# Modulation sums placed in layer 0, input sums with a margin, and silu as one ScalarE function

## The chip, the cores and the metric

The kernel runs on one core of one Trainium2 chip. A core has five engines that run side by side, each with its own queue of instructions in order: TensorE (PE, with its weight loads as PEld), VectorE (DVE), ScalarE (ACT), GpSimd (POOL) and SyncE (SP), which here issues the DMA transfers. The metric is the device time of one execution in microseconds (us); before the change it is 1677.81 us, the median of three runs.

## What is computed

Two layers of a transformer block act on two streams of 256 tokens, `x` and `ctx`. Each layer is a feed-forward, a mixing step (attention and pooling), and a second feed-forward; in the last layer `ctx` stops before the second half. Norms are scaled and shifted by modulation vectors, which come from a matrix of 1024 x 9216 in each layer.

```python
def rms_norm(x, g):
    xf = x.astype(jnp.float32)
    y = xf * lax.rsqrt(jnp.mean(xf * xf, axis=-1, keepdims=True) + RMS_EPS)
    return (y * g.astype(jnp.float32)).astype(x.dtype)

def modulate(h, shift, scale):
    return h * (1.0 + scale) + shift

def mod_vectors(cvec, w_mod, b_mod):
    m = jax.nn.silu(cvec) @ w_mod + b_mod
    return jnp.split(m, N_MOD, axis=-1)

def swiglu(h, w_gate_up, w_down):
    gate, up = jnp.split(h @ w_gate_up, 2, axis=-1)
    return (jax.nn.silu(gate) * up) @ w_down

def sandwich_ffn(x, w_gate_up, w_down, g_pre, g_post, shift, scale, gate):
    h = modulate(rms_norm(x, g_pre), shift, scale)
    return x + 0.5 * gate * rms_norm(swiglu(h, w_gate_up, w_down), g_post)
```

`D_MODEL` is 1024, `D_FF` 2816 (22 blocks of 128), `N_MOD` 9, `DEPTH` 2.

## The kernel before

**Numbers as pairs.** Each operand of a matmul is kept as a high and a low part; a product is three matmuls (`mm3`). To split a tile, ACT copies the high part and DVE subtracts it from the source to get the low part (`split`). Weights arrive by DMA in `raw` tiles of 1 MB and become two `w` tiles each (`Stream.prep`), so every weight costs one ACT and one DVE pass.

**Stages.** `ffn(0, 0)`, `token_mix(0)`, `ffn(0, 1)`, `ffn(1, 0)`, `token_mix(1)`, `ffn(1, 1)` run one behind the other. A feed-forward goes through its 22 blocks in groups (8, 8 and 6; in `ffn(1, 0)` 4, 4, 4, 4 and 6). Each group first makes the gate and up sums of its blocks (`pg`, `pu`) and their products (`product`, then `split` into `g`), and then multiplies `g` by the down weights into `pd`, which is added to `y`. Behind the last group, `close` does the norm of a token tile and prepares the next stage's input `h`; POOL takes the powers of the norms (`power`, `rs`).

**Seven products.** `ffn(1, 0)`, layer 1's first feed-forward, computes most blocks with seven quarter products in place of eight (`gate_up_seven`). It needs sums of weight quarters, which POOL makes from `raw` (`prep_seven`: `s12`, `s34`), and sums of input quarters, also on POOL (`Input.add_up`: from `yg` tiles, split into `ht`). Its first three blocks use the plain product, by halves of the tokens (`columns_half`). The quarter products land in banks `p1`, `p26`, `p57`, `p34` and are put together by DVE in `u` and `c`.

**Modulation.** The vectors of layer 0 for the first norm are made at the start by PE. All others are 16 jobs of nine steps (`mod_steps`): eight times a load of 0.5 MB (`wm`) and a multiply-add on DVE for each stream into `acc`, then `last`: DMAs that fold `acc` into `part`, three additions on POOL, a small matmul (`pm`) and, for gates, a transpose (`pr`). The last four jobs, of layer 1's second half, have one stream. `fill(rate)` behind each block of a feed-forward releases `rate` further steps; `debt` carries the fraction. There are 144 steps; 22 blocks at 2.6 release 57.

**What sets the order.** The whole program is first recorded and then ordered by a planner (`Recorder.order`): each engine's next instruction is the one that could start first by the planner's own prices, ties broken by the recorded order. `rec.margin` adds a time to the moment from which an instruction counts as ready. The order is fixed when the program is built; on the chip every engine takes its queue in that order and waits on semaphores. Places are limited: 16 large tiles (`w`, `g`, `h`), 2 `raw`, 10 working tiles (`wm`, `acc`, `part`, `tt`, `s12` among them), 8 PSUM banks.

All instructions of the recorded program carry one line number in the profile, L382 (`issue`), so groups are told apart by tile names.

Of the kernel before, what the change touches and what calls it, by code (L numbers as in the profile page):

```python
# [13 lines left out]
AF = mybir.ActivationFunctionType  # L14
ALU = mybir.AluOpType
# [10 lines left out]
EPS = 1e-6  # L26
# [9 lines left out]
LEAD = 3  # L36
# [1 line left out]
BLOCK = 4  # L38
PLACES = {"big": 16, "raw": 2, "wk": 10, "ps": 8, "st": 24}
LIMITS = {"ps": 1}  # L40
RATE = 2.6
BEHIND = 0
MARGIN = 6.0
HASTE = 0.5
# [4 lines left out]
XS, CS, ALL = slice(0, S), slice(S, N_TOK), slice(0, N_TOK)  # L49
# [350 lines left out]
def tile_dit_block(  # L400
# [36 lines left out]
    def wtile(shape, base="wk", dtype=F32):  # L437
        return rec.tile("wk", shape, dtype, base)
# [18 lines left out]
    class Stream:  # L457
        def __init__(self):
            self.plan = []
            self.ready = []  # L460
            self.raws = []
            self.taken = 0
            self.ahead = AHEAD

        def add(self, src, parts, seven=False):
            self.plan.append((src, parts, seven))
# [23 lines left out]
        def prep_seven(self, raw):  # L490

            (a11, a12), (a21, a22) = ((raw[:, i, 0:512], raw[:, i, 512:D]) for i in range(2))
            s12, s34 = wtile([P, 2, 512], "s12"), wtile([P, 2, 512], "s34")
            nc.gpsimd.tensor_add(s12[:, 0, :], a21, a22)
            nc.gpsimd.tensor_sub(s12[:, 1, :], s12[:, 0, :], a11)
            nc.gpsimd.tensor_sub(s34[:, 0, :], a11, a21)
            nc.gpsimd.tensor_sub(s34[:, 1, :], a12, s12[:, 1, :])
            wa = slot([P, 2, D], "w")
            split(wa[:, 0, :], wa[:, 1, :], raw[:, 0, :])
            w12 = slot([P, 2, D], "w")  # L500
            split(w12[:, 0, :], w12[:, 1, :], s12.rearrange("p a c -> p (a c)"))
            self.ready.append((wa, w12))
            w34 = slot([P, 2, D], "w")
            split(w34[:, 0, :], w34[:, 1, :], s34.rearrange("p a c -> p (a c)"))
            wb = wtile([P, 2, 512], "wb", F32R)
            split(wb[:, 0, :], wb[:, 1, :], a22)
            self.ready.append((w34, wb))
# [201 lines left out]
    def fill(n):  # L709

        debt[0] += n
        rec.delay = BEHIND
        while debt[0] >= 1 and todo:
            steps = todo[0][1]
            steps.pop(0)()
            debt[0] -= 1
            if not steps:
                todo.pop(0)
        rec.delay = 0
# [18 lines left out]
    def power(sq, eps):  # L738

        st = stat(2, "rs")  # L740
        nc.gpsimd.tensor_scalar(
            out=st[:, 0:1], in0=sq[:, 0:1], scalar1=sq[:, 1:2], scalar2=eps, op0=ALU.add, op1=ALU.add
        )
        nc.gpsimd.tensor_tensor(out=st[:, 1:2], in0=st[:, 0:1], in1=nhalf, op=ALU.pow)
        return st[:, 1:2]
# [4 lines left out]
    class Input:  # L750
# [21 lines left out]
        def add_up(self):  # L772

            self.sums = [slot([P, 2, 4, S], "ht") for _ in range(4)]
            lower, upper = slice(0, 4), slice(4, KD)
            for o in range(2):
                one, two = self.full[ORDER[o]], self.full[ORDER[2 + o]]
                a, b, c, d = one[:, lower, :], two[:, lower, :], two[:, upper, :], one[:, upper, :]
                nc.gpsimd.tensor_sub(a, b, a)
                nc.gpsimd.tensor_sub(b, c, b)  # L780
                nc.gpsimd.tensor_sub(c, c, a)
                nc.gpsimd.tensor_sub(d, d, c)
                for i, src in enumerate((a, c, b, d)):
                    dst = self.sums[i][:, :, :, o * P : (o + 1) * P]
                    split(dst[:, 0], dst[:, 1], src)
            self.full = {}
# [65 lines left out]
    def close(t, pd, y, half, nxt, Hn):  # L852

        n = wtile([P, D], "n")
        yg = wtile([P, D], "yg")
        sq, sx = stat(2, "sq"), stat(2, "sx")
        rec.haste = HASTE
        for h, hc in enumerate(HALVES):
            src = pd[h]
            if y is not None:  # L860
                src = y[:, hc]
                nc.vector.tensor_add(src, src, pd[h])
            square(n[:, hc], src, sq[:, h : h + 1], 1.0 / 16.0 if half else 1.0 / 32.0)
            nc.vector.tensor_mul(yg[:, hc], src, gbc[t // 2][:, hc])
        r = power(sq, 16.0 * EPS if half else EPS)
        for h, hc in enumerate(HALVES):
            nc.vector.scalar_tensor_tensor(
                out=X[t][:, hc], in0=yg[:, hc], scalar=r, in1=X[t][:, hc], op0=ALU.mult, op1=ALU.add
            )
            if nxt is None:  # L870
                nc.sync.dma_start(out=out[0, t * P : (t + 1) * P, hc], in_=X[t][:, hc])
            else:
                square(n[:, hc], X[t][:, hc], sx[:, h : h + 1])
        if nxt is not None:
            normed(t, nxt[0], nxt[1], n, yg.rearrange("p (k c) -> p k c", k=KD), Hn, sx)
        rec.haste = 0.0
# [45 lines left out]
    def ffn(l, ff, both, nxt, rate, lead, parts):  # L922
# [12 lines left out]

        def product(tt, pg, pu):

            nc.scalar.activation(tt[:, 0, :], pg, AF.Tanh, scale=0.5)
            nc.vector.scalar_tensor_tensor(out=tt[:, 1, :], in0=tt[:, 0, :], scalar=1.0, in1=pg, op0=ALU.add, op1=ALU.mult)
            nc.vector.tensor_mul(tt[:, 0, :], tt[:, 1, :], pu)  # L940

        def gate_up_evac(f, pg, pu):
# [7 lines left out]
        def gate_up(fs, parts):  # L950
            held = []
            for f in fs:
                held.append((f, ws.get(), ws.get(), bank("pg"), bank("pu")))
            for part in parts:
                for f, wg, wup, pg, pu in held:
                    if seven:
                        columns_half(pg, wg, part)
                        columns_half(pu, wup, part)
                    else:
                        columns(pg, wg, part)  # L960
                        columns(pu, wup, part)
                    if part is parts[-1]:
                        gate_up_evac(f, pg, pu)
                if seven and part is parts[0]:
                    H["now"].add_up()

        def gate_up_seven(f):

# [43 lines left out]
        for gi, (f0, f1) in enumerate(groups):  # L1012
            f = f0
            if gi == 0 and parts is None:
                by_token()
                f = BLOCK
            elif gi == 0:
                gate_up(tuple(range(lead)), parts)
                f = lead
                fill(lead * rate)  # L1020
            while f < f1:
                if seven:
                    gate_up_seven(f)
                else:
                    gate_up((f,), (cs,))
                f += 1
                fill(rate)
            if gi + 1 < len(groups):
                for h in range(2):
                    hc = slice(h * 512, (h + 1) * 512)  # L1030
# [342 lines left out]

    ffn(0, 0, True, (0, 3), RATE, START, (CS, XS))
    token_mix(0, (0, 6))
    ffn(0, 1, True, (1, 0), RATE, LEAD, (CS, XS))
    ffn(1, 0, True, (1, 3), RATE, LEAD, (0, 1))
    token_mix(1, (1, 6))
    ffn(1, 1, False, None, 0.0, 0, None)

    with tc.manual_schedule():
        rec.issue(tc.nc, rec.order(), {tag: psum if tag == "ps" else pool for tag in PLACES})
# [103 lines left out]
```

## Time and profile before

| | us |
|---|---|
| median of 3 runs | 1677.81 (1677.76 to 1678.05) |
| the profiled execution's own time | 1681.01 |
| its span, first to last instruction | 1679.1 |

The stages in the profiled execution, as the first matmuls of each in PE's timeline show them:

| stage | begins about, us |
|---|---|
| `ffn(0, 0)` | 38 |
| `token_mix(0)` | 401 |
| `ffn(0, 1)` | 606 |
| its second and third group | 743 and 876 |
| `ffn(1, 0)` | 982 (its first seven-product block 1021) |
| `token_mix(1)` | 1347 |
| `ffn(1, 1)` | 1483 |

A row of a group or a timeline names the engine, the operation, and `out<-in` by tiles with buffer numbers left out; `[4.76 <-ACT g_big L382]` means that the engine stood idle for 4.76 us before it and that ACT's writing of `g` ended the wait. Matmuls are pipelined and their ends are modelled, so time lost on PE is better read from the distance between starts than from its busy share.

### The profile page before, as it was taken

Reading aid. Unit: us, or ns where it says so; the run is one execution under the profiler, and the core shown is the slowest. Engines: PE = TensorE matmul, PEld = TensorE weight load, DVE = VectorE, ACT = ScalarE, POOL = GpSimd, SP = SyncE. Lnnn points to the kernel's source line nnn. Section 1 sums busy time; section 2 is a strip of 40 time slices with the busy share of each in tenths; the row PEclk is TensorE's granted clock in tenths of the full one; section 3 lists DMA queues with packets and bytes.
Section 4 is the critical chain, followed back from the end, with each engine's and each line's share of the span. In section 5 each row is a group of like instructions: output and inputs, shape, how many; then the busy total and the mean of one; then the engine's idle time right before and its main releaser. Section 6 shows DMA issues by size and latency. Waiting matters only on the chain.

```text
span 1679.1 us, 23648 instructions
## 1 busy us (share of the span) xinstructions
PE 1624.4 (97%) x9074; PEld 1396.6 (83%) x9074; DVE 1276.3 (76%) x1748; ACT 729.0 (43%) x1287; POOL 363.7 (22%) x348
## 2 busy tenths in 40 slices
PE   6999999999999999999999988999999999899998
PEld 4988888888877798888888888979889888779997
DVE  7987876556789689967745499899989788975664
ACT  7422322225566562232222273433434567664442
POOL 1011111102133211120110064362754022210000
PEclk9999999999999999999999999999999999999999
DMA  9467656631222425765554216354323412355551
GB/s 377 165 233 245 226 176 217 200 104 66 89 73 86 158 101 206 249 212 202 197 187 164 100 42 230 132 187 168 121 101 105 163 57 100 123 199 191 201 197 57
DMA packets 98960, 269.11 MB, mean 160 GB/s; under 512 B 9424, under 2 KB 39328, under 8 KB 87072
## 3 DMA queue, kind: packets, MB, share of 16 engines
q1 hardware_dynamic: 98848, 267.60, 45.7%
q8 instruction: 72, 1.18, 0.3%
q14 instruction: 40, 0.33, 0.1%
HBM read 251.80 MB, written 1.09 MB: 151 GB/s over the span
## 4 chain that ended last, share of the span: by engine, by line
PE 74%; DVE 12%; ACT 5%; issue 3%; DMA 2%; POOL 2%; SPq 1%; POOLq 0%; DVEq 0%; ACTq 0%
PE pd_ps L382 22%; PE pg_ps L382 19%; PE pu_ps L382 19%; PE p_ps L382 6%; DVE w_big L382 3%; PE pk_ps L382 2%; PE pv_ps L382 2%; ACT n_wk L382 2%; POOL rs_st L382 2%; PE pq_ps L382 1%; DVE acc_wk L382 1%; DMA w_big<-in_wmod_dram 1%; ACT sx_wk L382 1%; DVE tt_wk L382 1%; PE pt_ps L382 1%
## 5 line engine op out<-in xcount | busy, mean ns | idle before, releaser
L382 DVE TENSOR_TENSOR w_big<-raw_raw,w_big 128x1024 fp32r<-128x1024 f32 x293 | 374.5, 1291 | 103.2 <-ACT w_big L382 102.5
L382 PE MATMUL pd_ps<-w_big,g_big 128*128 128x512 f32 x1848 | 437.6, 397 | 9.9 <-ACT g_big L382 7.0
L382 PEld LDWEIGHTS pd_ps<-w_big,g_big 128*128 128x128 f32 x1848 | 347.9, 189 | 91.5 <-ACT g_big L382 7.9
L382 ACT ACTIVATE w_big<-raw_raw 128x1024 fp32r<-128x1024 f32 x293 | 302.6, 1053 | 230.9 <-DMA raw_raw<-in_wgu_dram 92.2
L382 PE MATMUL pu_ps<-h_big,w_big 128*128 128x512 f32 (+1 forms) x1944 | 367.8, 342 | 0.0
L382 PEld LDWEIGHTS pu_ps<-h_big,w_big 128*128 128x128 f32 x1944 | 305.6, 189 | 42.6
L382 PE MATMUL pg_ps<-h_big,w_big 128*128 128x512 f32 (+1 forms) x1752 | 331.0, 343 | 2.6 <-ACT h_big L382 1.7
L382 PEld LDWEIGHTS pg_ps<-h_big,w_big 128*128 128x128 f32 x1752 | 276.0, 189 | 43.6 <-ACT h_big L382 2.6
L382 DVE SCALAR_TENSOR_TENSOR acc_wk<-wm_wk,csil,acc_wk 128x1024 f32<-128x1024 f32 x196 | 249.5, 1307 | 41.4 <-DMA wm_wk<-in_wmod_dram 41.3
L382 POOL TENSOR_TENSOR part_wk<-part_wk 128x512 f32<-128x512 f32 (+2 forms) x84 | 89.5, 1066 | 474.6 <-DMA part_wk<-acc_wk 380.8
L382 ACT ACTIVATE g_big<-tt_wk 128x512 fp32r<-128x512 f32 (+1 forms) x84 | 49.2, 585 | 285.5 <-DVE tt_wk L382 283.5
L382 POOL TENSOR_SCALAR rs_st<-sq_st 128x1 f32<-128x1 f32 x24 | 8.3, 346 | 521.0 <-ACT n_wk L382 520.9
L382 POOL TENSOR_TENSOR s_wk<-raw_raw 128x512 f32<-128x512 f32 x38 | 67.4, 1784 | 92.3 <-DMA raw_raw<-in_wgu_dram 39.9
L382 PE MATMUL p_ps<-h_big,w_big 128*128 128x256 f32 x684 | 86.7, 280 | 0.0
L382 PE MATMUL p_ps<-ht_big,w_big 128*128 128x256 f32 x684 | 84.1, 281 | 0.0
L382 PEld LDWEIGHTS p_ps<-h_big,w_big 128*128 128x128 f32 x684 | 83.5, 189 | 0.3
L382 PEld LDWEIGHTS p_ps<-ht_big,w_big 128*128 128x128 f32 x684 | 82.2, 189 | 0.0
L382 ACT ACTIVATE tt_wk<-pg_ps 128x512 f32<-128x512 f32 (+1 forms) x67 | 35.9, 536 | 96.2 <-PE pg_ps L382 73.9
L382 DVE TENSOR_TENSOR g_big<-tt_wk,g_big 128x512 fp32r<-128x512 f32 (+1 forms) x84 | 59.4, 707 | 21.3 <-ACT g_big L382 21.1
L382 DVE TENSOR_TENSOR y_big<-y_big,pd_ps 128x512 f32<-128x512 f32 x72 | 47.1, 680 | 36.0 <-PE pd_ps L382 36.0
L382 PE MATMUL pd_ps<-w_big,mix_big 128*128 128x512 f32 x288 | 72.0, 399 | 0.5 <-DVE mix_big L382 0.5
L382 DVE SCALAR_TENSOR_TENSOR tt_wk<-tt_wk,pg_ps 128x512 f32<-128x512 f32 (+1 forms) x67 | 41.0, 612 | 34.1 <-ACT tt_wk L382 33.6
(159 smaller groups left out, 1851.0 us busy)
## 6 DMA issues: line engine op xcount, KB each, us to landing
raw_raw<-in_wgu_dram SPq DMA_DIRECT2D x84, 1024.0 KB, 4.9
wm_wk<-in_wmod_dram SPq DMA_DIRECT2D x128, 512.0 KB, 6.2
raw_raw<-in_wdn_dram SPq DMA_DIRECT2D x44, 1024.0 KB, 5.1
part_wk<-acc_wk SPq DMA_DIRECT2D x224, 64.0 KB, 2.5
raw_raw<-in_wkq_dram SPq DMA_DIRECT2D x8, 1024.0 KB, 4.7
raw_raw<-in_wout_dram SPq DMA_DIRECT2D x8, 1024.0 KB, 4.9
w_big<-in_wmod_dram SPq DMA_DIRECT2D x7, 1024.0 KB, 12.6
gb_wk<-grow SPq DMA_DIRECT2D x10, 512.0 KB, 6.0
```

Source lines behind the costliest of these rows:

```text
L382: getattr(getattr(nc, op.engine), op.method)(*[self.real(a) for a in op.args], **{k: self.real(a) for k, a in op.kw.items()})
```

## The change

Layer 0's second feed-forward releases steps at 2.6, 4.2 and 5.6 per block in its three groups, which brings the sum to all 144 steps; layer 1's feed-forwards release none. `product` takes silu in one ACT function, so `tt` is half of what it was, and the norm's epsilon behind it is a quarter of what it was. The first of POOL's sums for the first seven-product block, and the first of the input sums for each pair of token tiles, get a margin in the planner, and `add_up` is recorded one block later.

```diff
-RATE = 2.6
+RATE = (2.6, 2.6, 2.6)
+LATER = (2.6, 4.2, 5.6)
+NONE = (0.0,) * 5
...
             s12, s34 = wtile([P, 2, 512], "s12"), wtile([P, 2, 512], "s34")
+            rec.margin = 0.0 if self.sevens else 2 * MARGIN
+            self.sevens += 1
             nc.gpsimd.tensor_add(s12[:, 0, :], a21, a22)
+            rec.margin = 0.0
             nc.gpsimd.tensor_sub(s12[:, 1, :], s12[:, 0, :], a11)
...
                 one, two = self.full[ORDER[o]], self.full[ORDER[2 + o]]
+                rec.margin = MARGIN
                 a, b, c, d = one[:, lower, :], two[:, lower, :], two[:, upper, :], one[:, upper, :]
                 nc.gpsimd.tensor_sub(a, b, a)
+                rec.margin = 0.0
...
-        r = power(sq, 16.0 * EPS if half else EPS)
+        r = power(sq, 4.0 * EPS if half else EPS)
...
-            nc.scalar.activation(tt[:, 0, :], pg, AF.Tanh, scale=0.5)
-            nc.vector.scalar_tensor_tensor(out=tt[:, 1, :], in0=tt[:, 0, :], scalar=1.0, in1=pg, op0=ALU.add, op1=ALU.mult)
+            nc.scalar.activation(tt[:, 1, :], pg, AF.Silu)
             nc.vector.tensor_mul(tt[:, 0, :], tt[:, 1, :], pu)
...
-                for f, wg, wup, pg, pu in held:
+                for i, (f, wg, wup, pg, pu) in enumerate(held):
+                    if seven and part is parts[1] and i == 1:
+                        H["now"].add_up()
...
-                if seven and part is parts[0]:
-                    H["now"].add_up()
...
-                fill(lead * rate)
+                fill(lead * rate[gi])
...
-                fill(rate)
+                fill(rate[gi])
...
-    ffn(0, 1, True, (1, 0), RATE, LEAD, (CS, XS))
-    ffn(1, 0, True, (1, 3), RATE, LEAD, (0, 1))
+    ffn(0, 1, True, (1, 0), LATER, LEAD, (CS, XS))
+    ffn(1, 0, True, (1, 3), NONE, LEAD, (0, 1))
     token_mix(1, (1, 6))
-    ffn(1, 1, False, None, 0.0, 0, None)
+    ffn(1, 1, False, None, NONE, 0, None)
```

The diff doesn't show what the planner makes of it. Three places follow, of before (L382) and of the change (L384); the four digits in a name tell buffers apart.

The first place is DVE in `ffn(1, 0)`, from the putting together of the first seven-product block (`c`, `u`) to its product `tt`, ahead of the first group's down-projection. Before:

```order
L382 SCALAR_TENSOR_TENSOR acc_wk_8205<-wm_wk_8311,csil,acc_wk_8205 128x1024
L382 TENSOR_TENSOR col_100<-pm_ps_8388,colt 128x8
L382 TENSOR_TENSOR u_wk_8344<-p_ps_8367,c_wk_8383 128x512
L382 TENSOR_TENSOR col_100<-col_100,colt 128x8
L382 TENSOR_TENSOR w_big_8300<-raw_raw_8097,w_big_8300 128x1024
L382 TENSOR_TENSOR c_wk_8383<-p_ps_8367,u_wk_8344 128x256
L382 TENSOR_TENSOR w_big_8319<-raw_raw_8097,w_big_8319 128x1024
L382 TENSOR_TENSOR c_wk_8383<-p_ps_8400,u_wk_8344 128x512
L382 TENSOR_TENSOR w_big_8430<-raw_raw_8371,w_big_8430 128x1024
L382 SCALAR_TENSOR_TENSOR tt_wk_8455<-tt_wk_8455,c_wk_8383 128x512
L382 TENSOR_TENSOR wb_wk_8441<-raw_raw_8371,wb_wk_8441 128x512
L382 TENSOR_TENSOR tt_wk_8455<-tt_wk_8455,c_wk_8383 128x512
```

And now, from the same block's first `c` to its `g`:

```order
L384 TENSOR_TENSOR c_wk_8447<-p_ps_8410,u_wk_8414 128x2x256
L384 TENSOR_TENSOR wb_wk_8440<-raw_raw_8376,wb_wk_8440 128x512
L384 TENSOR_TENSOR u_wk_8414<-p_ps_8444,c_wk_8447 128x512
L384 TENSOR_TENSOR c_wk_8447<-p_ps_8444,u_wk_8414 128x256
L384 TENSOR_TENSOR wb_wk_8482<-raw_raw_8422,wb_wk_8482 128x512
L384 TENSOR_TENSOR w_big_8494<-raw_raw_8376,w_big_8494 128x1024
L384 TENSOR_TENSOR c_wk_8447<-p_ps_8475,u_wk_8414 128x512
L384 TENSOR_TENSOR tt_wk_8525<-tt_wk_8525,c_wk_8447 128x512
L384 TENSOR_TENSOR g_big_8406<-tt_wk_8525,g_big_8406 128x512
```

The sums `acc` and the column `col` are gone, and between the last `c` and `g` stands one operation where there were four (two of them, `w` and `wb`, for later blocks).

The second place is DVE in `ffn(0, 1)`, in the second group's down-projection, whose first half ends with four additions to `y`. Before:

```order
L382 TENSOR_TENSOR y_big_6074<-y_big_6074,pd_ps_6865 128x512
L382 TENSOR_SCALAR acc_wk_7011<-wm_wk_6974,csil 128x1024
L382 TENSOR_TENSOR y_big_6074<-y_big_6074,pd_ps_6872 128x512
L382 TENSOR_TENSOR y_big_6086<-y_big_6086,pd_ps_6880 128x512
L382 TENSOR_TENSOR y_big_6086<-y_big_6086,pd_ps_6884 128x512
L382 TENSOR_TENSOR w_big_7021<-raw_raw_6899,w_big_7021 128x1024
L382 TENSOR_TENSOR w_big_7055<-raw_raw_6969,w_big_7055 128x1024
L382 TENSOR_TENSOR w_big_7061<-raw_raw_6969,w_big_7061 128x1024
L382 TENSOR_TENSOR w_big_7087<-raw_raw_7040,w_big_7087 128x1024
```

And now, from the third of those additions:

```order
L384 TENSOR_TENSOR y_big_6062<-y_big_6062,pd_ps_6900 128x512
L384 TENSOR_TENSOR y_big_6062<-y_big_6062,pd_ps_6904 128x512
L384 TENSOR_TENSOR w_big_7053<-raw_raw_6910,w_big_7053 128x1024
L384 SCALAR_TENSOR_TENSOR acc_wk_6932<-wm_wk_7007,csil,acc_wk_6932 128x1024
L384 TENSOR_SCALAR acc_wk_7083<-wm_wk_7011,csil 128x1024
L384 SCALAR_TENSOR_TENSOR acc_wk_7083<-wm_wk_7047,csil,acc_wk_7083 128x1024
L384 TENSOR_TENSOR w_big_7096<-raw_raw_7003,w_big_7096 128x1024
L384 TENSOR_TENSOR w_big_7105<-raw_raw_7003,w_big_7105 128x1024
L384 SCALAR_TENSOR_TENSOR acc_wk_7083<-wm_wk_7085,csil,acc_wk_7083 128x1024
L384 TENSOR_TENSOR w_big_7137<-raw_raw_7076,w_big_7137 128x1024
```

Sums now stand between the weights of this stretch: 19 between the second group's last product and the third group's first, where there were four.

The third place is ACT in `token_mix(0)` at the first head's exponentials, with the semaphores that a row waits for. Before:

```order
L382 ACTIVATE w_big_3535<-raw_raw_3302 128x1024
L382 ACTIVATE v_big_3512<-pv_ps_3509 128x512 [waits PE_49]
L382 ACTIVATE sc_wk_3580,sc_st_3569<-pC_ps_3556,sc_st_3569 128x256 [waits DVE_49,PE_49,Activation_49]
L382 ACTIVATE sx_wk_3552,sm_st_3553<-sx_wk_3552,sm_st_3553 128x256 [waits DVE_49]
L382 ACTIVATE sc_wk_3580,sc_st_3569<-pC_ps_3556,sc_st_3569 128x256
```

And now:

```order
L384 ACTIVATE w_big_3513<-raw_raw_3280 128x1024
L384 ACTIVATE v_big_3490<-pv_ps_3487 128x512 [waits PE_49]
L384 ACT_TABLE_LOAD [waits DVE_49,PE_49]
L384 ACTIVATE sc_wk_3558,sc_st_3547<-pC_ps_3534,sc_st_3547 128x256 [waits Activation_49]
L384 ACTIVATE sx_wk_3530,sm_st_3531<-sx_wk_3530,sm_st_3531 128x256 [waits DVE_49]
```

A table load has come in between the waits and the first exponential. The program had one table load and has six now: the others stand at the start, ahead of the first product of `ffn(0, 0)`, of `ffn(0, 1)` and of `ffn(1, 1)`, and ahead of the first exponential of `token_mix(1)`, there with no wait on it.

More of the change, by code (lines that the diff above doesn't have):

```diff
@@ L463, in __init__ @@
             self.ahead = AHEAD
+            self.sevens = 0
         def add(self, src, parts, seven=False):
```

## The prediction

> **What bounds the kernel now.** I read the page's busy shares first, then the windows by stage, then the waits of PE, and last PE's and DVE's timelines where PE waits.
>
> ```profile
> PE 1624.4 (97%) x9074; PEld 1396.6 (83%) x9074; DVE 1276.3 (76%) x1748; ACT 729.0 (43%) x1287; POOL 363.7 (22%) x348
> ```
>
> PE is busy 97% of the span, and the change leaves its matmuls as they are. Only the rest can go, so the question is where it lies. The windows (busy us of PE, PEld, DVE, ACT, POOL; clock; DMA share; GB/s) give it by stage; the granted clock is 0.96 or more in all of them.
>
> ```profile
> 0.00:38.00 38.00, 23.44 (x153) 16.57 (x154) 26.59 (x44) 27.83 (x48) 4.46 (x18) 0.96 0.95 373
> 606.00:743.00 137.00, 136.65 (x742) 117.45 (x742) 117.60 (x126) 46.35 (x69) 22.65 (x24) 1.00 0.61 212
> 743.00:943.70 200.70, 200.70 (x883) 164.00 (x882) 122.77 (x133) 53.61 (x67) 17.38 (x18) 1.00 0.51 176
> 943.70:1021.50 77.80, 73.51 (x465) 65.48 (x464) 62.55 (x83) 40.94 (x84) 30.58 (x28) 0.98 0.29 101
> 1021.50:1193.90 172.40, 162.35 (x1057) 146.52 (x1056) 157.82 (x158) 64.58 (x89) 91.05 (x55) 0.97 0.48 165
> 1193.90:1347.00 153.10, 152.72 (x1080) 142.08 (x1078) 131.95 (x153) 68.86 (x103) 57.86 (x38) 1.00 0.35 122
> ```
>
> The same windows for the modulation sums `acc` alone (DVE's busy us and their number):
>
> ```profile
> 943.70:1021.50 77.80, 5.86 (x5) 0.98 0.29 101
> 1021.50:1193.90 172.40, 31.95 (x21) 0.97 0.48 165
> 1193.90:1347.00 153.10, 0.00 (x0) 1.00 0.35 122
> ```
>
> Layer 0's second feed-forward (606 to 944) loses nothing on PE. Layer 1's first one (from 1021) loses 10.0 us while modulation is still in it and 0.4 us after its last sum: the same code on the same kind of blocks, with DVE at 92% and at 86%. Four down-projections of 96 matmuls lie there, which I call D1 to D4:
>
> ```profile
> 1031.56 5.28 PE L382 MATMUL pd_ps<-w_big,g_big 128*128 128x512 f32 x22
> ...
> 1044.93 16.64 PE L382 MATMUL pd_ps<-w_big,g_big 128*128 128x512 f32 x60 [4.76 <-ACT g_big L382]
> 1061.41 0.87 PE L382 MATMUL p_ps<-h_big,w_big 128*128 128x256 f32 x6
> ...
> 1101.26 8.51 PE L382 MATMUL pd_ps<-w_big,g_big 128*128 128x512 f32 x36
> 1112.00 0.73 PE L382 MATMUL pd_ps<-w_big,g_big 128*128 128x512 f32 x2 [2.23 <-ACT g_big L382]
> ...
> 1129.47 0.75 PE L382 MATMUL p_ps<-h_big,w_big 128*128 128x256 f32 x5
> ...
> 1169.21 7.77 PE L382 MATMUL pd_ps<-w_big,g_big 128*128 128x512 f32 x33
> ...
> 1193.86 1.36 PE L382 MATMUL p_ps<-h_big,w_big 128*128 128x256 f32 x10
> ...
> 1233.48 8.96 PE L382 MATMUL pd_ps<-w_big,g_big 128*128 128x512 f32 x38
> 1242.66 13.65 PE L382 MATMUL pd_ps<-w_big,g_big 128*128 128x512 f32 x58 [0.21 <-DVE g_big L382]
> 1256.15 1.08 PE L382 MATMUL p_ps<-h_big,w_big 128*128 128x256 f32 x8
> ```
>
> From first row to the next product they take 29.85 (1031.56 to 1061.41), 28.21, 24.65 and 22.67 us. D4, behind the last modulation, is my measure of a clean one. Each of the others waits for `g`, the last block's product, which DVE and ACT make. DVE's timeline ahead of D1's wait shows why it is late:
>
> ```profile
> 1036.87 0.68 DVE L382 TENSOR_TENSOR c_wk<-p_ps,u_wk 128x512 f32<-128x512 f32 x1
> 1037.47 1.72 DVE L382 TENSOR_TENSOR w_big<-raw_raw,w_big 128x1024 fp32r<-128x1024 f32 x1
> 1039.11 1.77 DVE L382 SCALAR_TENSOR_TENSOR tt_wk<-tt_wk,c_wk 128x512 f32<-128x512 f32 x1
> 1040.81 1.75 DVE L382 TENSOR_TENSOR wb_wk<-raw_raw,wb_wk 128x512 fp32r<-128x512 f32 x1
> 1042.47 1.75 DVE L382 TENSOR_TENSOR tt_wk<-tt_wk,c_wk 128x512 f32<-128x512 f32 x1
> 1044.91 0.98 DVE L382 TENSOR_TENSOR g_big<-tt_wk,g_big 128x512 fp32r<-128x512 f32 x1 [0.70 <-ACT g_big L382]
> ```
>
> The block's matmuls end at 1031.6, where D1 begins, yet DVE takes up its `c` only at 1036.87: it works off a queue without a gap.
>
> **Part 1, modulation leaves this feed-forward: -14.7 us.** All 26 sums go (5 + 21, 5.86 + 31.95 = 37.8 us of DVE), and with them their loads, POOL's reductions and the small matmuls and transposes in D2 and D3. Of DVE's 157.8 us in the 172.4 us window 125.9 stay, 73%, less than the 86% at which D4 was clean. If D1 to D3 become like D4, they give 7.18 + 5.54 + 1.98 = 14.7 us. D1 by itself: without the queue `c` follows at about 1032; the new order has `c`, the one `tt` and `g` in a row, at most 0.7 + 1.75 + 1.0 us, with two steps of ACT (silu and `g`) of about 0.6 us between, which is 1036.6; D1 reaches this block after 36 matmuls, at 1040.2. So 3.6 us are to spare. Bounds: all of the loss over D4 as the most, 0 if what stretches these operations to 1.75 us keeps DVE late without the queue too.
>
> **Part 2, the sums go to layer 0's second feed-forward: 0.** There are 26 more in 743 to 943.7, and silu takes 14 operations of 0.68 us away. DVE goes from 122.8 to 122.8 + 37.8 - 9.6 = 151.0 of 200.7 us, 75%, less than the 86% of 606 to 743, where PE lost 0.35 us. In the new order the five fullest blocks of the second group hold 30 sums, 6 weight splits and 5 products between them:
>
> ```profile
> L382 DVE SCALAR_TENSOR_TENSOR tt_wk<-tt_wk,pg_ps 128x512 f32<-128x512 f32 x49 | 33.5, 683 | 26.3 <-ACT tt_wk L382 26.1
> L382 DVE SCALAR_TENSOR_TENSOR acc_wk<-wm_wk,csil,acc_wk 128x1024 f32<-128x1024 f32 x196 | 249.5, 1307 | 41.4 <-DMA wm_wk<-in_wmod_dram 41.3
> L382 DVE TENSOR_TENSOR w_big<-raw_raw,w_big 128x1024 fp32r<-128x1024 f32 x293 | 374.5, 1291 | 103.2 <-ACT w_big L382 102.5
> ...
> 832.50:876.40 43.90, 43.90 (x194) 36.06 (x193) 24.92 (x28) 11.97 (x12) 4.99 (x6) 1.00 0.51 173
> ...
> 743.01 5.52 PE pg_ps L382 x24
> ```
>
> That is 30 x 1.31 + 6 x 1.29 + 5 x 1.46 = 54 us beside 5 x 2 x 5.52 = 55 us of PE (gate and up, 24 matmuls each); the blocks behind are lighter, and 19 of the sums stand between that group's last product and the next group's first, around a down-projection in which DVE had 25 us of work in 44. PE's work covers it; without that cover all 37.8 us would show. Loads: 26 x 0.512 MB on top of 176 GB/s x 200.7 us = 35.3 MB make 48.6 MB, 242 GB/s, where 0 to 38 moved 373.
>
> **Part 3, silu: +1.2 us.** 67 products lose one DVE operation each; on PE's path that is in part 1 already, and elsewhere no row of PE's waits names `tt`. ACT's pass I price as the tanh pass it replaces, 0.591 us: a square of the same size from PSUM (`n_wk<-pd_ps`) takes 0.588, so the function hardly counts. New are five table loads, because tanh, silu and exp alternate.
>
> ```profile
> L382 ACT ACTIVATE tt_wk<-pg_ps 128x512 f32<-128x512 f32 x49 | 29.0, 591 | 79.5 <-PE pg_ps L382 57.2 <-issue 14.6 <-DVE acc_wk L382 5.6
> L382 ACT ACTIVATE n_wk<-pd_ps 128x512 f32<-128x512 f32 x12 | 7.1, 588 | 8.8 <-PE pd_ps L382 8.8
> L382 ACT ACT_TABLE_LOAD x1 | 1.3, 1283 | 0.7 <-PEq L1474 0.7
> 452.77 0.47 ACT L382 ACTIVATE sc_wk<-pC_ps,sc_st 128x256 f32<-128x256 f32 x1 [2.70 <-DVE sm_st L382]
> 455.52 0.60 PE L382 MATMUL pp_ps<-ident,sc_wk 128*128 128x128 f32 x4
> 1387.40 0.51 ACT L382 ACTIVATE sx_wk<-sx_wk,sm_st 128x256 f32<-128x256 f32 x1 [2.34 <-DVE sm_st L382]
> ```
>
> In layer 0's attention the load stands behind the waits for DVE and PE, so the 2.70 us of idle time don't hide it: the first exponentials come 1.28 us later and PE, back to back up to the transposes at 455.52, loses about 1.2. In layer 1 the load has no wait ahead of it and fits into the 2.34 us. The three before silu lie beside matmuls. Bounds: 0, or all five exposed, 6.4 us.
> [...]
>
> **Part 4, the held-back sums: 0.**
>
> ```profile
> 976.17 1.75 POOL L382 TENSOR_TENSOR s_wk<-raw_raw 128x512 f32<-128x512 f32 x1
> ...
> 983.82 0.30 POOL L382 TENSOR_SCALAR rs_st<-sx_st 128x1 f32<-128x1 f32 x1 [3.27 <-ACT n_wk L382]
> ```
>
> POOL's first sums of a weight block now stand one ahead of the third token tile's norm instead of three, with three behind it; the input's own sums keep their place on POOL behind the last norm. At most PE's whole idle time of 943.7 to 1021.5, 4.3 us, is to be had; at worst three sums of up to 1.8 us (5.4) delay the next norm, ahead of which POOL now idles 3.3 us, +2.
>
> **Sum.** -14.7 + 0 + 1.2 + 0 = -13.5 us. The profiled execution took 1681.0 us (span 1679.1, 1.9 around it) and would take 1667.5. It lies 3.2 us above the median shown, so the median goes from 1677.8 to **1664.3**.
>
> **Rivals.**
> - Half of D1 to D3's loss stays because POOL's sums of weights still stretch DVE (the 1.75 us rows lie beside them). For it: `wb` takes 1.75 there. Against: D4 and all of 1193.9 to 1347 run beside the same POOL sums without loss. -7.3 + 1.2: 1671.7.
> [...]
> - The held-back sums free the end of the feed-forward before: -13.5 - 4.3, 1660.0. Against: their order behind the last norm is unchanged.
> [...]
> - **Slower**: the moved loads share SP's queue with the weights. If the transfer rate stays at 212 GB/s, the most that a stretch with modulation shows, 48.6 MB take 229 us where PE has 200.7, and weights come 28 us late in all: 28 - 13.5, 1692.3. It decides from 242 GB/s downward. Against: those 212 used 0.61 of the DMA engines, so the ceiling is near 348.
> - That the change isn't what it says (a silu in two passes): ACT gains 40 us at 43% busy, time unchanged.
>
> **Chances.** Forecast 0.64 (its own range 1661 to 1669), half stays 0.13, held-back sums help 0.08, switches 0.05, transfers 0.10. A measurement here tells 0.2%, 3.4 us, from no change: faster 0.85, same 0.05, slower 0.10. The range leaves out the last two cases and runs from the held-back case to the half case with a little to spare: 1658 to 1673.
>
> **What would show it.** Right: D1 to D3 at about 22.7 us with waits for `g` under 0.5; PE busy all of 743 to 944 although DVE carries 75%; six table loads, one with PE waiting some 1.2 us for `pp` in layer 0's attention. Wrong: new PE waits for `w_big` or for DMA between 743 and 944; waits for `g` that stay; PE waits at each table load.

## The result, and the profile after

| | before | after |
|---|---|---|
| time, median (us) | 1677.93 (4 runs, 1677.76 to 1681.25) | 1661.59 (4 runs, 1660.71 to 1662.74) |
| ratio, 95% interval | | 0.9898 [0.9881, 0.9916] |
| profiled execution: time, span (us) | 1681.01, 1679.1 | 1662.74, 1661.0 |

The change takes 16.3 us off (predicted 13.5; 1661.6 where 1664.3 was forecast, inside 1658 to 1673). By the two profiled spans it is 18.1.

The same windows as before the change (busy us of PE, PEld, DVE, ACT, POOL with their counts; clock; DMA share; GB/s), from the profile after:

```profile
743.00:943.70 200.70, 200.68 (x885) 163.55 (x883) 142.20 (x147) 51.94 (x67) 31.55 (x30) 1.00 0.71 253
943.70:1021.50 77.80, 72.95 (x464) 65.36 (x465) 59.81 (x80) 42.70 (x87) 28.67 (x28) 0.98 0.17 61
1021.50:1193.90 172.40, 172.40 (x1189) 159.87 (x1188) 127.95 (x135) 72.26 (x96) 83.38 (x48) 1.00 0.30 104
```

PE idled 10.05 us in the last of them and now idles in none of it. DVE fell there from 157.8 to 128.0 us; the prediction had 125.9. In 743 to 944 DVE rose from 122.8 to 142.2 us and the transfers from 176 to 253 GB/s, and PE still loses nothing. The chain that ended last, after the change (start, us, what), has D1 to D4 one by one:

```profile
1031.87 22.27 PE pd_ps L384 x96
1054.14 39.60 PE p_ps L384 x336
1093.74 22.26 PE pd_ps L384 x96
1116.00 39.37 PE p_ps L384 x336
1155.37 22.17 PE pd_ps L384 x96
1177.54 39.70 PE p_ps L384 x336
1217.24 22.26 PE pd_ps L384 x96
```

The four take 88.96 us where they took 29.85 + 28.21 + 24.65 + 22.67 = 105.38: 16.4 us less. D1 now ends on time because the last block's product is made before PE comes to it. DVE's timeline there, after the change (start, us, engine, operation, idle time before it; busy time counts what an operation waits for while it runs, see the last section):

```profile
1031.55 2.31 DVE L384 TENSOR_TENSOR w_big<-raw_raw,w_big 128x1024 fp32r<-128x1024 f32 x1
1033.78 0.68 DVE L384 TENSOR_TENSOR c_wk<-p_ps,u_wk 128x512 f32<-128x512 f32 x1
1035.22 1.60 DVE L384 TENSOR_TENSOR tt_wk<-tt_wk,c_wk 128x512 f32<-128x512 f32 x1 [0.76 <-ACT tt_wk L384]
1037.51 1.02 DVE L384 TENSOR_TENSOR g_big<-tt_wk,g_big 128x512 fp32r<-128x512 f32 x1 [0.70 <-ACT g_big L384]
```

`c` comes at 1033.78 in place of 1036.87 and `g` is done at 1038.5. PE starts D1 at 1031.87 and reaches this block after 36 matmuls of 0.231 us, at 1040.2: 1.7 us to spare. One thing still stands ahead of `c`, the split of a weight, stretched to 2.31 us (it is the row `w_big_8494` of the new order).

The new table loads, from the groups after (busy time, mean ns of one, idle time ahead of them) and from the timeline of ACT and PE in layer 0's attention:

```profile
L384 ACT ACT_TABLE_LOAD x6 | 7.7, 1283 | 3.5 <-DVE sc_st L384 2.7 <-PEq L1481 0.7
```

```profile
450.97 1.28 ACT L384 ACT_TABLE_LOAD   x1 [2.69 <-DVE sc_st L384]
452.27 0.47 ACT L384 ACTIVATE sc_wk<-pC_ps,sc_st 128x256 f32<-128x256 f32 x1
454.51 0.63 PE L384 MATMUL pp_ps<-ident,sc_wk 128*128 128x128 f32 x4 [0.62 <-DVE sc_wk L384]
```

Six loads of 1283 ns, and only the one in layer 0's attention makes PE wait, 0.62 us. It stands behind 2.69 us of idle time, as foreseen, and the first exponential starts 0.02 us after it.

### The profile page after: what moved, and what is told of

Same layout as the page of the kernel before. It is cut to its first block, busy times and chain, and to the rows that moved or that the text cites. A ratio compares the mean times of both kernels' runs of the same rounds, so it can differ in the third digit from the quotient of the medians.

```text
span 1661.0 us, 23503 instructions
## 1 busy us (share of the span) xinstructions
PE 1615.6 (97%) x9074; PEld 1392.5 (84%) x9074; DVE 1211.8 (73%) x1662; ACT 736.4 (44%) x1292; POOL 355.7 (21%) x348
## 4 chain that ended last, share of the span: by engine, by line
PE 85%; DVE 6%; ACT 5%; POOL 2%; issue 1%; DMA 1%; SPq 0%; DVEq 0%; POOLq 0%; ACTq 0%
PE pd_ps L384 26%; PE pg_ps L384 19%; PE pu_ps L384 19%; PE p_ps L384 11%; PE pv_ps L384 2%; PE pk_ps L384 2%; ACT n_wk L384 2%; POOL rs_st L384 2%; PE pq_ps L384 1%; DVE w_big L384 1%; DMA w_big<-in_wmod_dram 1%; PE pt_ps L384 1%; PE po_ps L384 1%; PE pp_ps L384 1%; ACT sx_wk L384 1%
## 5 line engine op out<-in xcount | busy, mean ns | idle before, releaser
L384 DVE TENSOR_TENSOR w_big<-raw_raw,w_big 128x1024 fp32r<-128x1024 f32 x293 | 371.2, 1282 | 124.1 <-ACT w_big L384 123.6
L384 PE MATMUL pd_ps<-w_big,g_big 128*128 128x512 f32 x1848 | 431.5, 394 | 0.0
L384 PEld LDWEIGHTS pd_ps<-w_big,g_big 128*128 128x128 f32 x1848 | 345.8, 188 | 78.4 <-ACT grows L384 0.2
L384 ACT ACTIVATE w_big<-raw_raw 128x1024 fp32r<-128x1024 f32 x293 | 302.8, 1053 | 231.7 <-DMA raw_raw<-in_wgu_dram 103.6
L384 PE MATMUL pu_ps<-h_big,w_big 128*128 128x512 f32 (+1 forms) x1944 | 366.5, 341 | 0.0
L384 PEld LDWEIGHTS pu_ps<-h_big,w_big 128*128 128x128 f32 x1944 | 303.7, 188 | 42.3
L384 PE MATMUL pg_ps<-h_big,w_big 128*128 128x512 f32 (+1 forms) x1752 | 331.8, 344 | 3.8 <-DVE h_big L384 2.4
L384 PEld LDWEIGHTS pg_ps<-h_big,w_big 128*128 128x128 f32 x1752 | 277.1, 191 | 44.1 <-DVE h_big L384 2.9
L384 DVE SCALAR_TENSOR_TENSOR acc_wk<-wm_wk,csil,acc_wk 128x1024 f32<-128x1024 f32 x196 | 245.2, 1290 | 78.8 <-DMA wm_wk<-in_wmod_dram 78.5
L384 POOL TENSOR_TENSOR part_wk<-part_wk 128x512 f32<-128x512 f32 (+2 forms) x84 | 89.0, 1060 | 495.6 <-DMA part_wk<-acc_wk 466.6
L384 ACT ACTIVATE g_big<-tt_wk 128x512 fp32r<-128x512 f32 (+1 forms) x84 | 49.2, 586 | 273.2 <-DVE tt_wk L384 257.2
L384 POOL TENSOR_SCALAR rs_st<-sq_st 128x1 f32<-128x1 f32 x24 | 7.6, 316 | 448.0 <-ACT n_wk L384 447.9
L384 POOL TENSOR_TENSOR s_wk<-raw_raw 128x512 f32<-128x512 f32 x38 | 63.8, 1687 | 131.6 <-DMA raw_raw<-in_wgu_dram 94.2
L384 PE MATMUL p_ps<-h_big,w_big 128*128 128x256 f32 x684 | 86.9, 281 | 0.0
L384 PEld LDWEIGHTS p_ps<-h_big,w_big 128*128 128x128 f32 x684 | 83.7, 189 | 0.3
L384 PE MATMUL p_ps<-ht_big,w_big 128*128 128x256 f32 x684 | 83.3, 280 | 0.0
L384 PEld LDWEIGHTS p_ps<-ht_big,w_big 128*128 128x128 f32 x684 | 81.6, 189 | 0.0
L384 DVE TENSOR_TENSOR g_big<-tt_wk,g_big 128x512 fp32r<-128x512 f32 (+1 forms) x84 | 57.8, 688 | 29.9 <-ACT g_big L384 29.9
L384 PE MATMUL pd_ps<-w_big,mix_big 128*128 128x512 f32 x288 | 71.9, 399 | 0.5 <-DVE mix_big L384 0.5
L384 ACT ACTIVATE tt_wk<-pg_ps 128x512 f32<-128x512 f32 (+1 forms) x67 | 35.8, 534 | 75.3 <-PE pg_ps L384 62.4
L384 DVE TENSOR_TENSOR y_big<-y_big,pd_ps 128x512 f32<-128x512 f32 x72 | 47.9, 683 | 27.9 <-PE pd_ps L384 27.8
L384 DVE TENSOR_TENSOR w_big<-s_wk,w_big 128x1024 fp32r<-128x1024 f32 x38 | 55.8, 1468 | 16.5 <-ACT w_big L384 16.4
```

The lines of the kernel that those rows point to most:

```text
L384: getattr(getattr(nc, op.engine), op.method)(*[self.real(a) for a in op.args], **{k: self.real(a) for k, a in op.kw.items()})
```

## The experiments

Each was timed beside the kernel before on the same chip: e1 to e4 on one, e5 to e8, e9 to e11 and e12 on three others. D1 to D4 and the names are those of the prediction. "Idle" is PE's idle time in the window 1021.5 to 1250, which holds D1 to D3 and the start of D4: 10.3 us before the change, 0 after.

| kernel | median (us) | ratio to before [95%] | its before |
|---|---|---|---|
| e1 modulation moved, alone | 1665.27 | 0.9922 [0.9909, 0.9936] | 1678.57 |
| e2 silu, alone | 1673.06 | 0.9973 [0.9961, 0.9984] | 1678.57 |
| e3 held-back sums, alone | 1679.18 | 1.0001 [0.9993, 1.0010] | 1678.57 |
| e4 modulation and silu | 1660.47 | 0.9891 [0.9877, 0.9904] | 1678.57 |
| e5 the sums narrowed in place | 1667.29 | 0.9932 [0.9919, 0.9946] | 1678.63 |
| e6 e1 and idle sums on DVE | 1683.60 | 1.0028 [1.0018, 1.0038] | 1678.63 |
| e7 e4 with half moved back | 1664.95 | 0.9915 [0.9900, 0.9930] | 1678.63 |
| e8 e4 and an early exponential | 1666.79 | 0.9929 [0.9917, 0.9942] | 1678.63 |
| e9 e4 and one small copy | 1668.72 | 0.9943 [0.9928, 0.9957] | 1679.06 |
| e10 e8 and one copy | 1667.64 | 0.9939 [0.9924, 0.9954] | 1679.06 |
| e11 e8 and three copies | 1666.77 | 0.9931 [0.9915, 0.9948] | 1679.06 |
| e12 e8 without a new tile | 1662.74 | 0.9899 [0.9882, 0.9915] | 1679.39 |

### e1 to e4: the parts one by one

e1 is the kernel before with the rates alone:

```diff
-    ffn(0, 1, True, (1, 0), RATE, LEAD, (CS, XS))
-    ffn(1, 0, True, (1, 3), RATE, LEAD, (0, 1))
+    ffn(0, 1, True, (1, 0), LATER, LEAD, (CS, XS))
+    ffn(1, 0, True, (1, 3), NONE, LEAD, (0, 1))
```

> The kernel before with only the modulation steps moved (tanh and the order of the sums as before). Theory (the 26 sums' own time on DVE kept the last product g late at D1 to D3): nearly the whole gain, -14 to -16.5 us; D1 to D3 at 22.3 to 22.9 us each, waits of PE for g_big under 0.5, DVE's longer products with tanh still covered. Rival A (the shorter product chain of silu is what brings g in time): -5 to -9 us, D1 still 2 us or more over a clean one. Rival B (the profiled gain is mostly a faster start and the held-back sums): -3 us or less.

e2 has only the product (and the constant that goes with it):

```diff
-            nc.scalar.activation(tt[:, 0, :], pg, AF.Tanh, scale=0.5)
-            nc.vector.scalar_tensor_tensor(out=tt[:, 1, :], in0=tt[:, 0, :], scalar=1.0, in1=pg, op0=ALU.add, op1=ALU.mult)
+            nc.scalar.activation(tt[:, 1, :], pg, AF.Silu)
```

> The kernel before with only silu by ScalarE's function (modulation where it was, the sums' order as before). Theory (DVE's backlog): it takes 4 DVE operations of 0.7 to 1.8 us out of the queue ahead of each of D1 and D2, of which D1's c was 5.3 us late, so it gains a part: -3 to -8 us with +0.8 us for the one exposed table load in it; some wait for g_big stays at D1. Rival A (product chain): -8 us or more. Rival C (the modulation's loads, POOL reductions and small matmuls make the loss, not its DVE time): +1 to -2 us, D1 to D3 as in the kernel before.

e3 has only the margins of the first sums and the later call of `add_up`:

```diff
+            rec.margin = 0.0 if self.sevens else 2 * MARGIN
...
+                    if seven and part is parts[1] and i == 1:
+                        H["now"].add_up()
```

> The kernel before with only the held-back sums. Theory: within 2 us of the kernel before, the three waits at the end of layer 0's second feed-forward (1.3, 2.6 and 1.4 us) as they were. Rival B (it frees that end): -3 to -5 us, with the 2.6 us wait for h_big gone.

e4 is the changed kernel without those two.

> The changed kernel without the held-back sums. Theory: within 1.5 us of the changed kernel's 1661.6, that is -15 to -18 us against the kernel before. Rival B (the held-back sums carry a part of the gain): -12 to -14 us.

Measured: -13.3, -5.5, +0.6 (no difference by its interval) and -18.1 us. PE's waits in the window 1021.5 to 1250 (us in total, times, longest), first of e1, then of e2:

```profile
PE pd_ps L384 <- DVE g_big L384: 0.7, 1, 0.7
PE pd_ps L384 <- ACT g_big L384: 0.6, 1, 0.6
```

```profile
PE pd_ps L382 <- ACT g_big L382: 6.3, 3, 3.1
PE pd_ps L382 <- DVE g_big L382: 2.5, 3, 2.0
```

Moving the sums takes the waits for `g` from 9.9 to 1.3 us, silu alone only to 8.8. So the sums carry most of the gain and Rivals A and B fall, though e1's gain is 0.7 us short of what the theory had at the least and its D1 takes 24.15 us, 1.9 over a clean one; the held-back sums carry nothing, and e4's interval holds the changed kernel's ratio. But silu is worth 4.8 us on top of e1 (4.4 by the spans), where the prediction counted it as a cost of 1.2 with its relief inside D1 to D3. The windows show where: e1 idles 1.37 us in 1021.5 to 1250, e4 nothing; e1 idles 1.57 us in 743 to 943.7 (a matmul that waits for POOL's `part`, 1.2, and a transpose), e4 nothing; against it stands the table load, 0.6. That is 2.3. Of the rest 0.6 is PE's own pace in layer 0's first feed-forward (below, with e8) and 1.0 lies in layer 1's last one, 196.0 us from its first matmul to the end in e1 and 195.0 in e4; 0.5 has no place yet.

### e5 and e6: is it DVE's time?

e5 keeps each instruction of the kernel before in its place and makes 23 of the sums narrow; e6 takes e1 and gives DVE sums that need no POOL and no matmul, and no loads but two that fill their tiles once:

```diff
 (e5)
-                            out=acc[v], in0=wm, scalar=csil[:, k, v : v + 1], in1=acc[v], op0=ALU.mult, op1=ALU.add
+                            out=acc[v][:, 0:D:P], in0=wm[:, 0:D:P], scalar=csil[:, k, v : v + 1], in1=acc[v][:, 0:D:P],
 (e6)
+                for _ in range(3):
+                    nc.vector.scalar_tensor_tensor(
+                        out=extra[1], in0=extra[0], scalar=u[:, 0, 0:1], in1=extra[1], op0=ALU.mult, op1=ALU.add
+                    )
```

> The kernel before, every instruction in its place on every engine, but 23 of the 26 sums that DVE makes in layer 1's first feed-forward take 8 columns in place of 1024 (those modulations are left incomplete). Loads, POOL's reductions and the small matmuls stay. Theory (the sums' time on DVE is what makes g late): DVE has some 30 us less to do and the waits for g_big at D1 to D3 shrink to 3 us in all or less: -10 to -14 us. Rival C (the modulation's loads, its reductions on POOL or its small matmuls make the loss): within 3 us of the kernel before.

> The kernel with only the modulation moved (tanh kept), with 27 sums of 128x1024 put back on DVE in layer 1's first feed-forward, three in each of nine blocks, on two tiles that stay in place: no loads, no POOL work, no small matmuls come with them, and nothing reads their result. Theory (DVE's time alone does it): the loss is back, +8 to +15 us over the kernel with only the modulation moved (1665.3), waits for g_big again at D1 to D3. Rival C: within 3 us of it.

Measured: e5 -11.3 us, e6 +18.3 over e1. Waits of PE in 1021.5 to 1250 in e5, and in a second fence the group of its narrowed sums:

```profile
PE pd_ps L382 <- ACT g_big L382: 2.9, 2, 1.9
PE pd_ps L382 <- DVE g_big L382: 1.9, 3, 1.0
```

```profile
L382 DVE SCALAR_TENSOR_TENSOR acc_wk<-wm_wk,csil,acc_wk 128x8 f32<-128x8 f32 x23 | 11.8, 514 | 6.5 <-DMA wm_wk<-in_wmod_dram 6.5
```

The same waits in e6, and its sums (DVE's busy us and their number in that window):

```profile
PE pd_ps L384 <- ACT g_big L384: 7.4, 3, 2.9
PE pd_ps L384 <- DVE g_big L384: 3.3, 3, 1.5
```

```profile
1021.50:1250.00 228.50, 37.88 (x27) 0.99 0.28 97
```

Taking 22 us off DVE, with loads, reductions and small matmuls in place, removes half of the waits, and D1 to D3 take 72.2 us together (82.7 before, 68.6 in e1); giving 37.9 us back to DVE, with no reductions and no small matmuls, brings all of the waits back (10.7 us). So DVE's time is enough to make the loss, taking it off removes most of it, and Rival C falls. e6 differs from the modulation in more than that: its sums wait for the `u` of their block, and two of the ten working tiles stay taken. That wasn't tried apart.

Three numbers missed. A sum of 8 columns still took 514 ns on average, so e5 took 22 us from DVE and not 30 (the last section says why), and 4.8 us of waits stay where 3 were expected. And e6 lost 18.3 us by the medians, where 15 was the most expected. Its profiled run, the fastest of its ten and 6 us under their median, loses 12.3, with D2 and D3 at 28.6 us each (28.2 and 24.65 before); what makes the other 6 us isn't shown.

### e7: half of it

```diff
-LATER = (2.6, 4.2, 5.6)
+LATER = (2.6, 3.4, 4.1)
+SOME = (1.3,) * 5
...
-    ffn(1, 0, True, (1, 3), NONE, LEAD, (0, 1))
+    ffn(1, 0, True, (1, 3), SOME, LEAD, (0, 1))
```

> The changed kernel without the held-back sums, and with half of the moved modulation back in layer 1's first feed-forward (1.3 steps a block there, 3.4 and 4.1 in the feed-forward before). Theory as the prediction has it (a queue on DVE with some 3.6 us to spare at each product, DVE at 86 to 88%): most of the half costs nothing, 0 to +3 us over the kernel without the held-back sums (1660.5). Rival D (each sum beside the products costs its share): half of the loss that the modulation makes with silu in place (12.6 us between e2 and e4), +5 to +8 us.

Measured: 1664.95, 4.5 us over e4 on another chip (3.6 by the two profiled spans), and between the two expectations, so both miss. Its waits of PE in 1021.5 to 1250:

```profile
PE pd_ps L385 <- ACT g_big L385: 2.9, 1, 2.9
PE pd_ps L385 <- DVE g_big L385: 0.3, 1, 0.3
```

The loss lies at D1: both waits are there, and it takes 27.8 us, 5.5 more than a clean one. D2 and D3 are clean (22.2 and 22.4 us), with 7 sums left from 1045 to 1250 where the kernel before has 17. So a sum doesn't cost a share: each down-projection has a margin, and D1's gives out first, 1.7 us by the rows of the changed kernel and not the 3.6 that the prediction gave it.

### e8 to e12: the table load, and a pace that changed

e8 puts a single exponential ahead of the attention, into ACT's idle time:

```diff
         v_tile(1, wv4)
+        if full:
+            nc.scalar.activation(stat(1, "warm"), V[0][:, 1, 0, 0:1], AF.Exp)
```

> The changed kernel without the held-back sums, and with one exponential of 128x1 ahead of layer 0's attention, which takes the table load into 2.7 us in which ACT idles. Theory (the one exposed load costs what PE waits there, 0.8 us): -0.5 to -1.2 us against the kernel without it (1660.5), the wait of PE for sc_wk at 454 us gone, still six table loads. [...] Rival F (PE makes the time up at its next wait): no change.

The load went where it was meant to go, and PE's wait for `sc_wk` in layer 0's attention (0.62) is gone. Yet e8 is 6.3 us slower than e4: both expectations missed. PE's timeline shows it long before the added instruction. The first matmuls of 512 columns in layer 0's first feed-forward, and the start of its last down-projection: PE never waits between, the granted clock is 1.00, and PE has the same number of matmuls in all kernels. Before, e4 and e8 in this order:

```profile
64.12 5.68 PE L382 MATMUL pg_ps<-h_big,w_big 128*128 128x512 f32 x24
...
377.47 7.74 PE L382 MATMUL pd_ps<-w_big,g_big 128*128 128x512 f32 x33
```

```profile
63.46 5.68 PE L384 MATMUL pg_ps<-h_big,w_big 128*128 128x512 f32 x24
...
376.18 9.14 PE L384 MATMUL pd_ps<-w_big,g_big 128*128 128x512 f32 x39
```

```profile
64.06 5.70 PE L384 MATMUL pg_ps<-h_big,w_big 128*128 128x512 f32 x24
...
378.12 7.05 PE L384 MATMUL pd_ps<-w_big,g_big 128*128 128x512 f32 x30
```

313.35, 312.72 and 314.06 us. e1 has 313.35 and the changed kernel 312.71. So there are three paces. It isn't the chip: e7 ran on e8's chip and has 312.71. Three more kernels asked whether it is the length of ACT's program:

```diff
 (e9: no exponential; e10, e11: one and three such copies ahead of it)
+            spare = stat(8, "warm")
+            nc.scalar.activation(spare[:, 1:2], V[0][:, 1, 0, 0:1], AF.Copy)
```

> The changed kernel without the held-back sums (1660.5), and with one ScalarE copy of 128x1 in the place where e8 had its exponential: no table switch moves, the copy takes some 0.2 us of ACT's idle time and nothing reads its result. Open: e8 took away the wait of 0.8 us and yet came out 6 us slower, with PE's matmuls following one another at 231.5 ns where the kernel without it has 230.6 (512 columns, a stretch in which PE never waits, and that lies ahead of the added instruction). Theory G (one more instruction in ACT's program shifts the pace of PE everywhere): 1665 to 1668, with the wait for sc_wk (0.8 us) still there. Rival H (the exponential itself or the moved table load is what costs): 1660 to 1661.5.

> e8 with one such copy ahead of its exponential, so ACT's program is two instructions longer than e4's. Theory G: the pace depends on the count and may come back, 1659 to 1661 if it does; any value between 1659 and 1668 that goes with the pace of PE's matmuls in the stretch ahead fits it. Rival H: as e8, 1666 to 1667.5, whatever the pace.

> e8 with three such copies ahead of its exponential: four instructions more than e4. [...] Rival H: as e8, 1666 to 1667.5.

All three have the slow pace, 314.06 us in that stretch. e9 has no exponential and is slow, so Rival H falls, although e10 and e11 come out close to its numbers (1667.64 and 1666.77). The pace is the same with one, two or four instructions added; that any added instruction slows PE isn't ruled out yet. What the four kernels share is a new small tile. It changes the addresses in SBUF; the start (bytes) of the 16 large tiles, of e4 and of e8, from the two programs:

```
e4: 42496 50688 58880 67072 75264 87552 99904 108096 120512 136896 145088 153280 161472 169664 177856 194240
e8: 42496 50688 58880 67072 75264 87552 99904 108096 120544 136928 145120 153312 161504 169696 177888 194272
```

The upper eight stand 32 bytes higher in e8, off the multiples of 64 that all sixteen have in e4. Apart from the one instruction on ACT, the two programs have the same instructions in the same order on every engine. The last run has the exponential and no new tile:

```diff
-            nc.scalar.activation(stat(1, "warm"), V[0][:, 1, 0, 0:1], AF.Exp)
+            nc.scalar.activation(craw[:, 0, 0:1], V[0][:, 1, 0, 0:1], AF.Exp)
```

> As e8 (one exponential of 128x1 ahead of layer 0's attention, no held-back sums), but it writes into a small tile that is already there and no longer used, so that no tile changes its address. In e8 to e11 the new small tile made one of the rotating small places 64 bytes long in place of 32, which moves 8 of the 16 large tiles (weights and activations), both tiles for loaded weights and 6 of the 10 middle ones up by 32 bytes, off multiples of 64. Theory I (the addresses make PE's pace, 230.6 ns a matmul of 512 columns before and 231.5 behind; the load is worth the 0.8 us that PE waits): pace 230.6 ns, no wait for sc_wk at 454 us, 1659.3 to 1660.2, that is 0.3 to 1.2 us under the 1660.5 without the exponential. Rival J (an added instruction on ACT sets the pace, whatever its tile): 1665 to 1669, pace 231.5 ns.

e12's tiles start where e4's do. Its rows in that stretch and one of layer 0's second feed-forward, and in a second fence pieces of the chain that ended last (start, us, what):

```profile
62.22 5.68 PE L384 MATMUL pg_ps<-h_big,w_big 128*128 128x512 f32 x24
...
374.93 10.30 PE L384 MATMUL pd_ps<-w_big,g_big 128*128 128x512 f32 x44
...
895.51 0.27 PE L384 MATMUL pr_ps<-ident,col 128*8 128x128 f32 x1 [2.23 <-DVE col L384]
```

```profile
864.80 8.51 DMA wm_wk<-in_wmod_dram
874.56 5.65 DMA wm_wk<-in_wmod_dram
887.84 5.97 DMA wm_wk<-in_wmod_dram
```

The pace is back, 312.71 us: Theory I holds for it, and Rival J and what was left of Theory G fall. The time isn't the expected one: 1662.74, with runs from 1660.48 to 1664.35. In the profiled run a transpose of the moved modulation waited 2.23 us, because its sums had waited for their loads; its chain runs through the loads there, that of the changed kernel through PE alone. So the 0.6 us that e12 was to save could not be told from the spread, and no version here is shown to beat the changed kernel: e4 has the lowest median, 1660.47, but the intervals of their ratios overlap.

## Why the prediction was right, point by point

- **What bounds the kernel, and Part 1 (-14.7): right, and mis-sized by 1.7 us.** D1 to D4 gave 16.4 us. D4, the measure of a clean one, still held a small wait itself (0.21 in its row): it went from 22.67 to 22.26, and D1 to D3 came down to 22.2 to 22.3 and not to 22.67. e1, e5 and e6 show that it was DVE's time; a part of that time is DVE waiting for POOL (last section), and taking POOL's weight sums away instead wasn't tried. The working of D1 was off in one step: it set `c` at 1032 and `g` at 1036.6, but a weight's split of 2.31 us stands ahead of `c`, so 1.7 us were to spare, not 3.6. That the forecast held for D1 even so was in part luck: half of the margin it counted on wasn't there. Silu belongs into that margin: without it (e1) 1.3 us of waits stay.
- **Part 2 (0): right for the changed kernel's profile, too sure for every run.** PE idled 0.02 us in 743 to 943.7, at 142.2 us of DVE (151.0 predicted; the window got 24 more sums and 30.3 us of them, where 26 and 37.8 were counted) and 253 GB/s (242 predicted). But the cover is thin: e1 loses 1.57 us in that window and e12's profiled run 2.23 in one wait.
- **Part 3 (+1.2): the place right, the size wrong, and a gain left out.** One load of five is exposed, 0.62 us. The load's 1.28 us are all that the rows show of a switch: behind it the first exponential starts after 0.02, and in layer 0's first feed-forward, where ACT doesn't idle ahead of the load, a copy ends at 55.66, the load begins at 55.68 and the first silu at 56.97. What the term lacked is that silu is worth 4.8 us on top of the moved modulation (e4 against e1): 2.9 us in which PE still idles with tanh, and a pace of PE that is 0.2% faster, 0.64 us in the stretch above. Why silu brings that pace stays open.
- **Part 4 (0): right.** e3 is level with the kernel before, and e4 without these edits is not slower than the changed kernel; in 943.7 to 1021.5 PE idles 4.85 us in the changed kernel's profile and 3.81 in e4's. In e3 the wait only moved: a matmul of the modulation waits 2.3 us for POOL's reductions at D1.
- **The sum.** -13.5 predicted for the profiled execution, -18.1 measured by its span: -16.4 from D1 to D4, +0.6 the load, -0.6 the pace in layer 0's first feed-forward, -0.65 an earlier start (63.47 in place of 64.12 for the row above; chance of the run, since with the same program up to there e1 and e3 have 63.53 and 62.70 in place of 64.12), and -1.2 in layer 1's last feed-forward (196.1 to 194.9 us from its first matmul to the end); the rest balances to 0.2. By the medians it is 16.3.
- **The rivals.** Half stays: out, D1 to D3 are clean although POOL is busy 83.4 of 172.4 us beside them and DVE's operations are still stretched (1.60 and 2.31 us in the rows above; 0.69 and 1.22 with POOL idle). The stretch is there, the loss isn't, because the shorter queue leaves room for it. Held-back sums help: out (e3). Switches, at a chance of 0.05: out, of six loads of 1283 ns one makes PE wait, 0.62 us. Slower by transfers: out as a whole, since 253 GB/s were delivered, but its mechanism is what e12's profiled run shows, at 2.2 us.

## What to carry to other kernels

Look at the stage, not at the share of the whole: DVE was 76% busy over the span, and what cost 16 us was a queue of a few us ahead of three particular products, so work that nothing waits for goes where the consumer has slack. Count the margin at each consumer with all that stands ahead of it in the queue (a split of 2.31 us was missed here), and with what each operation waits for on another engine while it runs, because the loss starts where the margin ends and is not shared out evenly. And before a small added tile or instruction is judged by the time, compare a stretch that it can't touch: here it had moved the other tiles.

## What the runs showed of the hardware that was not expected

- **D1's wait cost more than its length.** In the kernel before, D1's wait of 4.76 us was followed by matmuls at a clock of 0.50 (busy us of PE, clock, DMA share, GB/s by stretch):

```profile
1041.00:1045.00 4.00, 0.07 (x1) 0.77 0.34 94
1045.00:1049.00 4.00, 4.00 (x9) 0.50 0.94 350
1049.00:1053.00 4.00, 4.00 (x16) 0.88 0.32 117
1053.00:1057.00 4.00, 4.00 (x19) 1.00 0.40 98
```

9 matmuls in 4 us, then 16, then 19. That is how 4.76 us of waiting became 7.6 of loss (29.85 against 22.27). A lower clock stood behind shorter waits too. In the changed kernel PE waits 2.42 us for `h_big`, up to 983.66, and its clock was 0.61 in the stretch that holds the end of that wait and the matmuls behind it (0.59 in 1115 to 1119 of the kernel before, behind D2's waits of 2.23 and 1.42):

```profile
983.00:987.00 4.00, 3.34 (x16) 0.61 0.00 0
```

- **PE's pace went with where the tiles start.** In e8, with 8 of 16 large tiles (and both tiles of loaded weights, and 7 of the 10 middle ones) 32 bytes off a multiple of 64, 313 us of matmuls took 1.35 us longer (314.06 against 312.71 in e12), and the kernels e8 to e11 are 6 to 8 us slower than e4 in all. Carried over to all of PE's 1624 us, 1.35 in 313 would be 7.0 us (an estimate). e12 has e8's exponential and e4's addresses, and e4's pace; which of the tiles it is, and why, wasn't tried.
- **The pace also differs between tanh and silu with the tiles' places the same** (313.35 and 312.71 us, the same in each kernel of either kind that was compared). The cause is open, and the addresses aren't ruled out, since the order of the program gives many tiles another of these places (607 of PE's first 2200 matmuls have other addresses in e2 than before the change).
- **DVE operations with two inputs in SBUF that began beside a POOL sum ended behind it.** The mean of 514 ns for a narrowed sum in e5 (against 1285 for 128x1024 in the same kernel) mixes two kinds. 14 of the 23 took 0.22 to 0.24 us, and no POOL sum touches them. The other 9 took 0.41 to 1.28 us; each began beside a POOL sum and ended 0.03 us behind the end of one. DVE's and POOL's rows (start, us), one of each kind:

```profile
1064.93 1.26 DVE L382 SCALAR_TENSOR_TENSOR acc_wk<-wm_wk,csil,acc_wk 128x8 f32<-128x8 f32 x1
1064.54 1.62 POOL L382 TENSOR_TENSOR s_wk<-s_wk,raw_raw 128x512 f32<-128x512 f32 x1
1078.33 0.23 DVE L382 SCALAR_TENSOR_TENSOR acc_wk<-wm_wk,csil,acc_wk 128x8 f32<-128x8 f32 x1
```

The stretched rows at D1 follow the same pattern, before the change (1.72 to 1.77 us) and after it (1.60 and 2.31): each ends 0.55 us (512 columns) or 1.1 us (1024) behind the end of a POOL sum. So do all 54 operations of this kind that begin beside a POOL sum in 1021.5 to 1250 before the change, and all 38 after it. `c` of 512 columns, which reads PSUM, stays at 0.68 to 0.69 us beside POOL's sums too. So a part of DVE's busy time in this stage goes with POOL's sums and reads as waiting for them. Ahead of D1's wait before the change, five rows (1034.70 to 1042.47) hold 4.8 us over the 1.21 and 0.68 that such operations take with POOL idle, as much as the wait of 4.76: without POOL's sums beside it, this queue might have been in time with the modulation still there. No run tried that.
